# Keeping the activations token-major: weights as the moving operand, 512 columns wide, in a two-layer decoder trunk

## The chip, the cores and the metric

The kernel runs on one core of one Trainium2 chip. The metric is the device time of one execution in microseconds (us); lower is better. The kernel before was timed three times, and the profile shows one further execution.

## What is computed

The reference is a small decoder: 256 tokens of width 2048, two layers, everything in float32. Cut to what matters:

```python
for i in range(2):
    hn = rmsnorm(h, norm_mix[i])
    # layer 0: trailing means over tokens (windows 2, 4, 8, 16), then one 512x512 product per channel group
    # layer 1: differential attention, 8 heads: q, k, v from w_qkv, two softmaxes per head, rmsnorm, w_o
    h = h + (pool_mixer(hn, ...) if i == 0 else diff_attention(hn, ...))
    hn = rmsnorm(h, norm_ffn[i])
    h = h + (silu(hn @ w_gate[i]) * (hn @ w_up[i])) @ w_down[i]      # 2048 -> 5632 -> 2048
return rmsnorm(h, final_norm)
```

The weights are read once; the profile shows 350.96 MB read from HBM.

## The kernel before

**Precision.** A float32 product is carried by three passes in float32r. A weight tile w is split into `whi` (a cast, by ScalarE, L83) and `wlo` (w minus `whi`, by VectorE, L84); an activation x is split the same way into two halves [xh | xl] of one tile (`split`, L121 to L124). The passes are wh·xh, wl·xh and wh·xl.

**Layout.** The residual x is held feature-major: 16 tiles of 128 features by 256 tokens (`x_sb`). A product takes a 128x128 weight tile as TensorE's stationary operand and streams the activations through it. `product` (L89) makes one output tile of 128 features by 256 tokens in one PSUM bank: per weight tile a "big" matmul (L95) streams the 512 columns [xh | xl] through `whi` into both halves of the bank, and a "small" one (L98) streams the 256 columns xh through `wlo` onto the left half. I call the two a pair. The halves are added later, by a copy on ScalarE and an add on VectorE (`join`, L173).

Two products are token-major already: the group products of the pooling mixer and the v projection. `token_product` (L139) holds 128 tokens of xh or xl stationary and streams 512 weight columns: three matmuls (L147, L148, L149) of 512 columns for each 128 tokens and 128 rows of weights.

**Order of the work.** `Stream.unit` (L76) loads weights in chunks of 512 KB through SyncE's queue, four buffers deep, and splits each chunk once it is needed. The program is written stage by stage; a scheduler in the tile framework then fixes one static order for each engine, and the engines meet through semaphores. The stages are:

- the start (L182 to L268): x is loaded feature-major. Group 0 of the mixer's four channel groups is multiplied in plain float32 (L221), the others by `token_product`; `group_mean` (L243) scales by the norm, applies the trailing means with matmuls against a band matrix (L251 to L253) and adds to x;
- a feed-forward block, `ffn` (L270), run twice: 44 output tiles of gate and of up (16 pairs each, L278 and L285), joined, scaled by the norm's row `r`, silu, product, split into the 44 tiles `hT`; then 16 tiles of down (44 pairs each, L298), added to x;
- attention: q and k by `product` (32 tiles, L340), scores, softmax, transposed probabilities `aT` (L323); then for each of four 512-column parts of v a `token_product` (L399), and behind it for the two heads of that part the product of probabilities and v (L405 to L407), a norm per head (L411 to L415: two squares, `rsqrt`, two scalings `o_n`), four transposes by TensorE (L419), and the split into the operand `oT`; then w_o by `product` (L425);
- the final norm and the store (L433 to L440).

The norms need sums over features, which lie on partitions here: `norm_scale` (L152) gets them by matmuls with a tile of ones (L157) and spreads the result over partitions by four more (L164).

PSUM has eight banks of 128x512: five (`acc`) hold products, three (`aux`) everything else.

Of the kernel before, what the change touches and what calls it, by code (L numbers as in the profile page):

```python
# [9 lines left out]
F32 = mybir.dt.float32  # L10
# [6 lines left out]
P = 128  # L17
S = 256
D = 2048
NK = D // P  # L20
DFF = 5632
NF = DFF // P
# [3 lines left out]
CU = 8  # L26
WARM = 10
PLAIN = 1
WINDOWS = (2, 4, 8, 16)
HALO = 16  # L30
# [3 lines left out]


@with_exitstack
def trunk_kernel(ctx, tc, x_t, gains, subln, lam_in, band, dist,
                 pool_w, w_qk, w_v, w_o, w_gate, w_up, w_down, out):
# [12 lines left out]
    acc_ps = ctx.enter_context(tc.tile_pool(name="acc_ps", bufs=5, space=PSUM))  # L51
    aux_ps = ctx.enter_context(tc.tile_pool(name="aux_ps", bufs=3, space=PSUM))

# [9 lines left out]

    x_all = resid.tile([P, NK, S], F32, name="x_all")
    x_sb = [x_all[:, k, :] for k in range(NK)]
    xg = [resid.tile([P, 2, S], F32R, name=f"xg{k}") for k in range(NK)]

    def f32(ap):
        return ap.bitcast(F32)

# [1 line left out]
    class Stream:  # L72
        def __init__(self, w):
            self.w, self.next, self.have = w, 0, {}

        def unit(self, u):  # L76
            c = u // CU
            if c not in self.have:
                raw = wraw.tile([P, CU * P], F32, name="raw")
                nc.sync.dma_start(out=raw, in_=self.w[c])  # L80
                hi = whl.tile([P, CU * P], F32R, name="whi")
                lo = whl.tile([P, CU * P], F32R, name="wlo")
                nc.scalar.copy(hi, raw)  # L83
                nc.vector.tensor_tensor(lo, raw, f32(hi), ALU.subtract)  # L84
                self.have = {c: (hi, lo)}
            hi, lo = self.have[c]
            return hi, lo, (u % CU) * P

    def product(stream, u0, acts):  # L89
        """One output tile: units u0.. of the stream against acts; a bank [left | right]."""  # L90
        ps = acc_ps.tile([P, 2, S], F32, name="acc")
        n = len(acts)
        for k, a in enumerate(acts):
            hi, lo, at = stream.unit(u0 + k)
            big = lambda: nc.tensor.matmul(  # L95
                ps.rearrange("p a s -> p (a s)"), hi[:, at:at + P],
                a.rearrange("p a s -> p (a s)"), start=(k == 0), stop=(k == n - 1))
            small = lambda: nc.tensor.matmul(  # L98
                ps[:, 0, :], lo[:, at:at + P], a[:, 0, :], start=False, stop=False)
            if k < n - 1:  # L100
                big()
                small()
            else:
                small()
                big()
        return ps

    def rsqrt(ss, n, cols):
        """(ss / n + eps) ** -0.5 of [128, cols] sums, with one Newton step behind the
        square root's table."""  # L110
        v, s, t, r = (tmp.tile([P, 8], F32, name=f"rs_{x}") for x in "vstr")
        v, s, t, r = v[:, :cols], s[:, :cols], t[:, :cols], r[:, :cols]
        nc.vector.tensor_scalar(v, ss, 1.0 / n, EPS, ALU.mult, ALU.add)
        nc.scalar.activation(s, v, AF.Sqrt)
# [3 lines left out]
        nc.vector.scalar_tensor_tensor(r, t, 1.5, s, ALU.add, ALU.mult)  # L118
        return r

    def split(dst, src, gain):  # L121
        """dst = [hi | lo] of src * gain (gain by partition)."""
# [3 lines left out]
    def square_sum(k, ssq):  # L126
        if k == 0:
            nc.scalar.activation(ssq, x_sb[k], AF.Square)
        else:
            sq = tmp.tile([P, S], F32, name="sq")  # L130
            nc.scalar.activation(sq, x_sb[k], AF.Square)
            nc.vector.tensor_tensor(ssq, ssq, sq, ALU.add)

    def add_residual(k, ps):
        t = tmp.tile([P, S], F32, name="res_t")
        nc.vector.tensor_tensor(t, ps[:, 0, :], x_sb[k], ALU.add)
        nc.vector.tensor_tensor(x_sb[k], ps[:, 1, :], t, ALU.add)

    def token_product(stream, u0, acts):  # L139
        """[tokens, 512] in two banks: acts stationary against 512 columns of the stream."""  # L140
        ps = [acc_ps.tile([P, 512], F32, name="acc") for _ in range(2)]
        n = len(acts)
        for k, a in enumerate(acts):
            hi, lo, at = stream.unit(u0 + 4 * k)
            for t in range(2):
                xh, xl = a[:, 0, t * P:(t + 1) * P], a[:, 1, t * P:(t + 1) * P]
                nc.tensor.matmul(ps[t], xh, hi[:, at:at + 512], start=(k == 0), stop=False)  # L147
                nc.tensor.matmul(ps[t], xh, lo[:, at:at + 512], start=False, stop=False)  # L148
                nc.tensor.matmul(ps[t], xl, hi[:, at:at + 512], start=False, stop=(k == n - 1))  # L149
        return ps  # L150

    def norm_scale(ssq, rows=True):  # L152
        """Each token's rsqrt(mean square): by partition [128, 2], and [128, S] on every one."""
        ps = aux_ps.tile([P, 512], F32, name="aux")
        for t in range(2):
            for i, sq in enumerate(ssq):
                nc.tensor.matmul(ps[:, 2 * t:2 * t + 2], sq[:, t * P:(t + 1) * P], ones[:, 0:2],  # L157
                                 start=(i == 0), stop=(i == len(ssq) - 1))
        col = rsqrt(ps[:, 0:4:2], D, 2)
        if not rows:  # L160
            return col, None
        bc = aux_ps.tile([P, 512], F32, name="aux")
        for t in range(2):
            nc.tensor.matmul(bc[:, t * P:(t + 1) * P], col[:, t:t + 1].broadcast_to([P, P]), ident, start=True, stop=True)  # L164
        return col, bc

    def row_scale(ssq):
        col, bc = norm_scale(ssq)
        r = tmp.tile([P, S], F32, name="r_row")
        nc.scalar.copy(r, bc[:, :S])  # L170
        return col, r

    def join(ps, name):  # L173
        """left + right halves of a bank, in SBUF."""
        c = tmp.tile([P, S], F32, name=f"{name}_c", tag="join_c")
        nc.scalar.copy(c, ps[:, 1, :])  # L176
        s = tmp.tile([P, S], F32, name=f"{name}_s", tag="join_s", bufs=3)
        nc.vector.tensor_tensor(s, ps[:, 0, :], c, ALU.add)  # L178
        return s

# [1 line left out]
    with tc.tile_pool(name="start", bufs=1, reuse_waits="tile") as st:  # L182
        band_sb = st.tile([P, 4, P + HALO + P], F32, name="band_sb")
        pool_stream = Stream(pool_w)
# [4 lines left out]
        wp = aux_ps.tile([P, 512], F32, name="aux")  # L189
# [3 lines left out]
        def load_x(k0, k1):  # L193
            nc.sync.dma_start(out=x_all[:, k0:k1, :], in_=x_t[:, k0 * S:k1 * S].rearrange("p (k s) -> p k s", s=S))

        # the first groups' products in plain float32, which wait for no split
        zp = [None] * 4
        x0 = st.tile([P, 4 * PLAIN, S], F32, name="x0")
        w0 = []

        def load_w(c):
            raw = st.tile([P, CU * P], F32, name=f"w_plain{c}")
            nc.sync.dma_start(out=raw, in_=pool_w[c])
            w0.extend([raw[:, 0:512], raw[:, 512:]])

        load_x(0, 1)
        load_w(0)
        load_x(1, 4)
        load_w(1)
        for g in range(1, 4):  # L210
# [303 lines left out]
```

## Time and profile before

| what | value |
|---|---|
| time, median of 3 runs | 1941.9 us (1940.9 to 1942.17) |
| the profiled execution: first to last instruction (its span) | 1939.9 us |
| difference between that span and the median time | 2.0 us |
| TensorE (PE) busy | 1923.3 us, 99% of the span |
| VectorE (DVE) busy | 1187.4 us, 61% |
| ScalarE (ACT) busy | 938.8 us, 48% |
| DMA | 354.86 MB, mean 183 GB/s |

A matmul's row in the profile lasts from its start to a modelled end, and rows of successive matmuls overlap; how fast TensorE goes is read from start to start. PEld is the loading of stationary operands, which runs beside the matmuls. `PEclk` is the clock that TensorE was granted, 1.00 being full speed. The engine names with a q (SPq, DVEq, PEq) are the engines' instruction queues. The execution's own device time was not recorded apart from its span, so the work below adds the 2.0 us between that span and the median.

### The profile page before, as it was taken

How to read it: one execution, taken by the hardware profiler on the slowest of the kernel's cores; microseconds unless marked ns; L12 is line 12 of the kernel's file. 1: busy time of each engine (PE TensorE's matmuls, PEld its weight loads, DVE VectorE, ACT ScalarE, POOL GpSimd, SP SyncE). 2: the span in 40 equal slices, each digit the busy share in tenths (PEclk: the TensorE clock that was granted, in tenths of full speed). 3: DMA queues.
4: the chain of work that ended last, by engine and by line, in shares of the span. 5: the costliest groups of instructions: out<-in, count | busy, mean ns of one | idle time of the engine just before them, and what ended most of it. 6: DMA issues, size and time to landing. Idle time of an engine off the chain costs nothing.

```text
span 1939.9 us, 27612 instructions
## 1 busy us (share of the span) xinstructions
PE 1923.3 (99%) x10786; PEld 1664.6 (86%) x10786; DVE 1187.4 (61%) x1722; ACT 938.8 (48%) x1379; POOL 0.7 (0%) x6
## 2 busy tenths in 40 slices
PE   9999999999999999999999999999999999999997
PEld 7888888888888888888888888888888888888886
DVE  7766666666655555666655676666666666555554
ACT  7544444454444444544455545454544445444442
POOL 0000000000000000000000000000000000000000
PEclk9999999999999999999999999999999999999999
DMA  6666666656666665555555466665666665666663
GB/s 203 193 186 187 189 184 190 185 184 188 186 190 185 189 190 187 174 174 174 175 178 168 160 188 182 188 185 186 185 189 183 190 187 185 187 190 188 186 188 115
DMA packets 99330, 354.86 MB, mean 183 GB/s; under 512 B 11264, under 2 KB 13568, under 8 KB 99200
## 3 DMA queue, kind: packets, MB, share of 16 engines
q1 hardware_dynamic: 97984, 352.01, 59.4%
q8 instruction: 84, 1.38, 0.3%
q10 hardware_dynamic: 1216, 1.10, 0.2%
q14 instruction: 46, 0.38, 0.1%
HBM read 350.96 MB, written 2.10 MB: 182 GB/s over the span
## 4 chain that ended last, share of the span: by engine, by line
PE 98%; DVE 1%; ACT 0%; DMA 0%; issue 0%; SPq 0%; DVEq 0%
PE acc L95 60%; PE acc L98 30%; PE acc L148 2%; PE acc L149 2%; PE acc L147 2%; PE aux L376 1%; DMA x_all<-x_t 0%; PE aux L419 0%; PE aux L252 0%; DVE y_out L437 0%; PE aux L405 0%; PE aux L251 0%; DVE wlo L84 0%; PE aux L406 0%; PE aux L407 0%; ACT sq_in L227 0%
## 5 line engine op out<-in xcount | busy, mean ns | idle before, releaser
L95 PE MATMUL acc<-xg,whi 128*128 128x512 f32 x3328 | 1164.3, 399 | 0.0
L84 DVE TENSOR_TENSOR wlo<-raw,whi 128x1024 fp32r<-128x1024 f32 x662 | 810.1, 1224 | 475.0 <-ACT whi L83 459.4
L83 ACT CAST whi<-raw 128x1024 fp32r<-128x1024 f32 x662 | 694.7, 1050 | 506.6 <-PE acc L95 436.9
L98 PE MATMUL acc<-xg,wlo 128*128 128x256 f32 x3328 | 902.4, 281 | 0.0
L95 PEld LDWEIGHTS acc<-xg,whi 128*128 128x128 f32 x3328 | 612.6, 188 | 134.2
L98 PEld LDWEIGHTS acc<-xg,wlo 128*128 128x128 f32 x3328 | 628.3, 189 | 20.0
L95 PE MATMUL acc<-h,whi 128*128 128x512 f32 x1408 | 492.1, 394 | 0.0
L98 PE MATMUL acc<-h,wlo 128*128 128x256 f32 x1408 | 390.5, 281 | 0.0
L95 PEld LDWEIGHTS acc<-h,whi 128*128 128x128 f32 x1408 | 262.6, 188 | 59.6
L98 PEld LDWEIGHTS acc<-h,wlo 128*128 128x128 f32 x1408 | 264.0, 188 | 2.9
L176 ACT COPY g_c<-acc 128x256 f32<-128x256 f32 x88 | 32.7, 372 | 166.8 <-PE acc L95 166.8
L176 ACT COPY u_c<-acc 128x256 f32<-128x256 f32 x88 | 32.7, 372 | 166.4 <-PE acc L95 166.4
L178 DVE TENSOR_TENSOR u_s<-acc,u_c 128x256 f32<-128x256 f32 x88 | 37.3, 424 | 92.0 <-ACT u_c L176 92.0
L178 DVE TENSOR_TENSOR g_s<-acc,g_c 128x256 f32<-128x256 f32 x88 | 37.3, 424 | 90.0 <-ACT g_c L176 90.0
L95 PE MATMUL acc<-oT,whi 128*128 128x512 f32 x256 | 89.2, 396 | 0.0
L98 PE MATMUL acc<-oT,wlo 128*128 128x256 f32 x256 | 69.1, 282 | 0.0
L147 PE MATMUL acc<-whi,xg 128*128 128x512 f32 x152 | 60.5, 400 | 2.6 <-ACT whi L83 2.6
L148 PE MATMUL acc<-wlo,xg 128*128 128x512 f32 x152 | 61.7, 406 | 0.7 <-DVE wlo L84 0.7
L149 PE MATMUL acc<-whi,xg 128*128 128x512 f32 x152 | 61.0, 401 | 0.0
L95 PEld LDWEIGHTS acc<-oT,whi 128*128 128x128 f32 x256 | 47.1, 188 | 9.9
L290 ACT CAST h<-h 128x256 fp32r<-128x256 f32 x88 | 35.8, 407 | 39.6 <-DVE h L289 39.6
L98 PEld LDWEIGHTS acc<-oT,wlo 128*128 128x128 f32 x256 | 48.1, 188 | 1.5
(109 smaller groups left out, 751.6 us busy)
## 6 DMA issues: line engine op xcount, KB each, us to landing
raw<-w_gate SPq DMA_DIRECT2D x176, 512.0 KB, 4.1
raw<-w_up SPq DMA_DIRECT2D x176, 512.0 KB, 3.7
raw<-w_down SPq DMA_DIRECT2D x176, 512.0 KB, 4.3
raw<-w_qk SPq DMA_DIRECT2D x64, 512.0 KB, 3.6
raw<-w_v SPq DMA_DIRECT2D x32, 512.0 KB, 3.6
raw<-w_o SPq DMA_DIRECT2D x32, 512.0 KB, 4.3
raw<-pool_w SPq DMA_DIRECT2D x6, 512.0 KB, 7.0
x_all<-x_t SPq DMA_DIRECT2D x3, 512.0 KB, 7.5
```

The costliest lines, as they stand in the source:

```text
L83: nc.scalar.copy(hi, raw)
L84: nc.vector.tensor_tensor(lo, raw, f32(hi), ALU.subtract)
L95: big = lambda: nc.tensor.matmul(ps.rearrange("p a s -> p (a s)"), hi[:, at:at + P], a.rearrange("p a s -> p (a s)"), start=(k == 0), stop ...
L98: small = lambda: nc.tensor.matmul(ps[:, 0, :], lo[:, at:at + P], a[:, 0, :], start=False, stop=False)
L147: nc.tensor.matmul(ps[t], xh, hi[:, at:at + 512], start=(k == 0), stop=False)
L148: nc.tensor.matmul(ps[t], xh, lo[:, at:at + 512], start=False, stop=False)
L149: nc.tensor.matmul(ps[t], xl, hi[:, at:at + 512], start=False, stop=(k == n - 1))
L176: nc.scalar.copy(c, ps[:, 1, :])
L178: nc.vector.tensor_tensor(s, ps[:, 0, :], c, ALU.add)
L290: nc.scalar.copy(hT[j][:, 0, :], h)
L376: nc.tensor.matmul(sc[:, :nk], qk[:, c, qb * P:(qb + 1) * P], qk[:, 2 + c, :nk], start=True, stop=True)
```

## The change

The residual becomes token-major: `x_tok`, [128 tokens, 2 token blocks, 2048]. All products except q and k take the form that only v and the mixer had: activations stationary, 512 weight columns moving. Line numbers in this section are those of the changed kernel.

- **Products.** `group` computes 256 tokens by two blocks of 512 columns, in four banks at once: C11, C12 (first 128 tokens, left and right columns), C21, C22 (the other tokens). One step takes 256 rows of weights, one load of 1 MB in place of two of 512 KB, and 24 matmuls of 512 columns (L164). Three weight buffers in place of four, each twice as large; a split is one instruction of 128x2048 (L110, L111). A constant `SEVEN` for another variant is empty here, so its branches don't run.
- **Banks.** The four sums of `group` always lie in banks 6, 4, 5 and 7 (C11, C12, C21, C22); `aux` rotates over 5, 6 and 7, `acc` (q, k, mixer) over 0 to 4.
- **Feed-forward.** Gate and up stand side by side, 512 columns of each per group, 11 groups a layer. The result `h` has tokens on partitions, so it is turned back by eight transposes per group (L361) before it is split (L363, L364). The 11 groups are taken in three parts (4, 4, 3), each followed by its part of down (two groups), which is added to `x_tok`.
- **Norms.** A token's sum of squares is now along the free axis: ScalarE squares with an accumulated sum (`square_sum`); no matmuls with ones. The scale is applied per partition.
- **Operands.** Where a block needs x as stationary operand, `transposed` turns it by TensorE, 8 transposes for each 512 columns (L236), and splits.
- **Attention.** v comes in two groups of 1024 columns in place of four of 512, and behind each stand four heads in place of two.
- **Start and end.** x is loaded twice: feature-major for the mixer's products (2 MB) and token-major (2 MB); the pool scale (1 MB) and the final gain come broadcast over partitions. The mean over tokens is a matmul of 512 columns against the band matrix. The output is stored token-major.

The diff, cut to its core:

```diff
-    wraw = ctx.enter_context(tc.tile_pool(name="wraw", bufs=4))
-    whl = ctx.enter_context(tc.tile_pool(name="whl", bufs=4))
+    wraw = ctx.enter_context(tc.tile_pool(name="wraw", bufs=3))
+    whl = ctx.enter_context(tc.tile_pool(name="whl", bufs=3))
...
+    def load(src):
+        raw = wraw.tile([P, 4, 512], F32, name="raw")
+        nc.sync.dma_start(out=raw, in_=src)
+        return raw
+
+    def halves(raw, lo_block=0):
+        hi = whl.tile([P, 4, 512], F32R, name="whi")
+        lo = whl.tile([P, 4, 512], F32R, name="wlo")
+        nc.scalar.copy(hi[:, lo_block:], raw[:, lo_block:])
+        nc.vector.tensor_tensor(lo[:, lo_block:], raw[:, lo_block:], f32(hi[:, lo_block:]), ALU.subtract)
+        return hi, lo
...
+    def group(steps, seven_pool=None):
...
+                plan.append([(C11, [((0, 0), 0, B11), ((1, 0), 0, B21)]), (C12, [((0, 0), 0, B12), ((1, 0), 0, B22)]),
+                             (C21, [((0, 1), 0, B11), ((1, 1), 0, B21)]), (C22, [((0, 1), 0, B12), ((1, 1), 0, B22)])])
...
+                        ah, al = (a[:, k, i, t * P:(t + 1) * P] for i in range(2))
+                    for x, y in ((ah, hi), (ah, lo), (al, hi)):
+                        left[b] -= 1
+                        nc.tensor.matmul(ps[b], x, y[:, block], start=first, stop=(left[b] == 0))
...
+    def square_sum(ss, t, j):
+
+        sq = tmp.tile([P, 512], F32, name="sq", bufs=1)
+        nc.scalar.activation(sq, x_tok[:, t, j * 512:(j + 1) * 512], AF.Square, accum_out=ss[:, t, j:j + 1])
...
+    def transposed(xp, j, gain, seven=()):
+
+        for p in (2 * j, 2 * j + 1):
+            ps = aux((P, 2, 2, P))
...
+                    nc.tensor.transpose(ps[:, i, at], x_tok[:, t, cols], ident)
...
+                    split(xp[p][:, i], ps[:, i].rearrange("p t s -> p (t s)"), g[i])
...
+            for c, n in enumerate(CHUNKS):
...
+                for g in range(g0, g0 + n):
+                    ps = group([(xq[p], p in seven, w_gu[layer][g, p]) for p in range(NP)], hp)
+                    cs = combined(ps, hp)
+                    h = hp.tile([P, 2, 512], F32, name="h")
+                    for t in range(2):
+                        a = cs[t][0] if seven else hp.tile([P, 512], F32, name="silu", bufs=2)
+                        nc.scalar.activation(a, cs[t][0], AF.Silu, scale=r[:, t:t + 1])
+                        nc.vector.scalar_tensor_tensor(h[:, t], cs[t][1], r[:, t:t + 1], a, ALU.mult, ALU.mult)
+                    for i in range(2):
+                        ht = hp.tile([P, 2, 2, S], F32R, name=f"h{g - g0}_{i}")
+                        tp = aux((P, 2, S))
...
+                        nc.scalar.copy(ht[:, :, 0], tp)
+                        nc.vector.tensor_tensor(ht[:, :, 1], tp, f32(ht[:, :, 0]), ALU.subtract)
...
+                    ps = group([(hp_tiles[i], False, w_down[layer][o, 2 * g0 + i]) for i in range(2 * n)])
...
+                            nc.vector.tensor_tensor(x_tok[:, t, cols], cs[t][b], x_tok[:, t, cols], ALU.add)
...
-        for c in range(4):
-            cols = slice(c * 512, (c + 1) * 512)
-            vp = token_product(v_stream, c * NK * 4, xg)
...
-            for h in (2 * c, 2 * c + 1):
+        for g in range(2):
+            cs = combined(group([(xp[p], False, w_v[g, p]) for p in range(NP)]))
...
+            for h in range(4 * g, 4 * g + 4):
```

How the change moves TensorE's instructions is shown at two places. The first is the seam between one gate and up product and the next. In the kernel before, the next product (another `acc` bank) follows the last pair directly; this is the seam of two output tiles in the first feed-forward block, xg14 and xg15 being the last two feature tiles and xg0 the first.

```order
L95 MATMUL acc_1506<-xg14_102,whi_1531 128x512
L98 MATMUL acc_1506<-xg14_102,wlo_1532 128x256
L98 MATMUL acc_1506<-xg15_103,wlo_1532 128x256
L95 MATMUL acc_1506<-xg15_103,whi_1531 128x512
L95 MATMUL acc_1558<-xg0_88,whi_1561 128x512
L98 MATMUL acc_1558<-xg0_88,wlo_1562 128x256
```

In the changed kernel, TensorE at the first such seam of the first feed-forward block (b7_484 is C22 of the group that ends, h_701 its result, b4_737, b7_751, b5_744 and b6_730 are C12, C22, C21 and C11 of the next group; xp_93 and xp_94 are its first two steps):

```order
L164 MATMUL b7_484<-whi_673,xp_100 128x512
L361 MATMUL b5_709<-ident_77,h_701 128x128
L361 MATMUL b6_717<-ident_77,h_701 128x128
L164 MATMUL b4_737<-whi_726,xp_93 128x512
L164 MATMUL b4_737<-wlo_727,xp_93 128x512
L164 MATMUL b4_737<-whi_726,xp_93 128x512 x2
L361 MATMUL b5_709<-ident_77,h_701 128x128 x3
L361 MATMUL b6_717<-ident_77,h_701 128x128 x3
L164 MATMUL b4_737<-wlo_727,xp_93 128x512
...
L164 MATMUL b7_751<-whi_726,xp_93 128x512
...
L164 MATMUL b5_744<-whi_726,xp_93 128x512
```

Eight transposes now stand between the products, and the next group starts in the one bank (4) that they do not use; banks 5 and 6 follow once the transposed `h` has been read out of them.

The second place is behind a v product. Before, TensorE goes on with the next part of v (acc_9631, acc_9632) while a head is on its way through ScalarE and VectorE: the head's products with v (L405 to L407), twenty v matmuls, then the head's transposes (L419).

```order
L149 MATMUL acc_9420<-whi_9549,xg15_103 128x512
L147 MATMUL acc_9631<-whi_9635,xg0_88 128x512
L405 MATMUL aux_9567<-v_sb_7304,aT0_7686 128x256
L406 MATMUL aux_9567<-v_sb_7304,aT0_7686 128x256
L407 MATMUL aux_9567<-v_sb_7304,aT0_7686 128x256
L148 MATMUL acc_9631<-wlo_9636,xg0_88 128x512
...
L149 MATMUL acc_9631<-whi_9653,xg3_91 128x512
L419 MATMUL aux_9589<-ident_80,o_n_9586 128x128
L405 MATMUL aux_9599<-v_sb_7304,aT1_7946 128x256
```

In the changed kernel, TensorE behind the first v group (b7_6812 is its C22; b4_7174 is C12 of the second v group, the only bank of it that the heads leave free, taken three steps ahead):

```order
L164 MATMUL b7_6812<-whi_7001,xp_438 128x512
L517 MATMUL b5_7033<-v_sb_4861,aT0_5204 128x256
...
L517 MATMUL b7_7065<-v_sb_4861,aT1_5440 128x256
...
L164 MATMUL b4_7174<-whi_7227,xp_433 128x512
L531 MATMUL b6_7055<-ident_77,o_n_7052 128x128 x4
L531 MATMUL b5_7087<-ident_77,o_n_7084 128x128 x4
L517 MATMUL b6_7097<-v_sb_4861,aT2_5676 128x256
...
L517 MATMUL b5_7129<-v_sb_4861,aT3_5912 128x256
...
L531 MATMUL b7_7119<-ident_77,o_n_7116 128x128 x4
L531 MATMUL b6_7151<-ident_77,o_n_7148 128x128 x4
L164 MATMUL b5_7181<-whi_7163,xp_431 128x512
```

Eighteen matmuls of bank 4 stand between the first two heads' products and their transposes; between those and the transposes of heads 2 and 3 stand only the products of these heads, and none of the v product.

More of the change, by code (lines that the diff above doesn't have):

```diff
@@ L69, in f32 @@
         return ap.bitcast(F32)
[L72 to L87, printed above, removed]
@@ L139, in token_product @@
[L139 to L150, printed above, removed]
@@ L152, in norm_scale @@
[L152 to L165, printed above, removed]
@@ L188, in trunk_kernel @@
         nc.scalar.activation(warm[:, 0:1], ones[:, 0:1], AF.Sqrt)
[L189 removed]
+        wp = aux()
         for _ in range(WARM):
@@ new lines, in trunk_kernel @@
+        load_x(1, 4)
+        nc.sync.dma_start(out=w0[:, 2:4], in_=pool_w[0][:, 2:4])
+        load_x(4, 8)
+        x0 = st.tile([P, 4, S], F32, name="x0")
+        zp = [None] * 4
+        zp[0] = [acc() for _ in range(2)]
+        for k in range(4):
+            nc.vector.tensor_scalar(x0[:, k, :], xf[:, k], gain_sb[:, 0, k:k + 1], None, ALU.mult)
+            for t in range(2):
+                nc.tensor.matmul(zp[0][t], x0[:, k, t * P:(t + 1) * P], w0[:, k], start=(k == 0), stop=(k == 3))
@@ L333, in transpose_probs @@
             aT.append(a_t)
+        acts = [tile_of(xp, k) for k in range(NK)]
         probs = None
@@ L443, in _chunks @@
-def _chunks(w):
-    return w.reshape(P, -1, CU * P).transpose(1, 0, 2)
+                    split(oT[h][:, e], tp[:, e, :], gs[:, e:e + 1])
+        xq = operand(SEVEN)
+        for g in range(2):
+            cs = combined(group([(oT[p], False, w_o[g, p]) for p in range(NP)]))
+            for b in range(2):
+                j = 2 * g + b
+                cols = slice(j * 512, (j + 1) * 512)
+                for t in range(2):
+                    nc.vector.tensor_tensor(x_tok[:, t, cols], cs[t][b], x_tok[:, t, cols], ALU.add)
+                    square_sum(ss_next, t, j)
+                transposed(xq, j, 4, SEVEN)
```

476 lines of the change are left out of this document (279 added, 197 removed).

## The prediction

> **What bounds the kernel now.** I read the page first: engine shares and the chain that ended last.
>
> ```profile
> span 1939.9 us, 27612 instructions
> PE 1923.3 (99%) x10786; PEld 1664.6 (86%) x10786; DVE 1187.4 (61%) x1722; ACT 938.8 (48%) x1379; POOL 0.7 (0%) x6
> PE 98%; DVE 1%; ACT 0%; DMA 0%; issue 0%; SPq 0%; DVEq 0%
> ```
>
> TensorE is the chain for 98% of the span; nothing else is worth a stage's time. What counts is how fast its matmuls follow each other, and where it will have to wait. Pairs first, by the big matmul of each pair, in three clean stretches (gate and up, down, w_o; columns: stretch, length, busy and count of PE, of PEld, clock, DMA):
>
> ```profile
> 1192.00:1655.00 463.00, 456.62 (x1311) 240.54 (x1311) 1.00 0.62 186
> 1692.00:1915.00 223.00, 221.88 (x636) 118.36 (x636) 1.00 0.60 184
> 1100.00:1178.00 78.00, 76.91 (x223) 40.73 (x223) 1.00 0.62 189
> ```
>
> A pair takes 463/1311 = 0.3532 us in gate and up, 223/636 = 0.3506 in down, 78/223 = 0.3498 for w_o. The form that replaces them stands in the same trace: the v product, here the first and the last of 45 matmuls in a row without a gap in the timeline.
>
> ```profile
> 999.63 0.39 PE L148 MATMUL acc<-wlo,xg 128*128 128x512 f32 x1
> ...
> 1009.60 0.39 PE L147 MATMUL acc<-whi,xg 128*128 128x512 f32 x1
> ```
>
> 44 steps in 9.97 us: 0.2266 us for 512 columns. A pair is worth 1.5 of them, 0.340 us.
>
> **The change part by part.** *Products.* Gate and up are 2 x 88 x 16 = 2816 pairs, down 2 x 16 x 44 = 1408, w_o 256: 2816 x 0.3532 + 1408 x 0.3506 + 256 x 0.3498 = 1577.8 us. After: 280 steps of 24 matmuls, 6720 x 0.2266 = 1522.8. **-55 us.** This is the firm gain; q, k and v keep their matmuls. The Trainium skill, "TensorE: Matmul & The Clock Gate", section "Back-to-back issue gap", gives an isolated gap of N/2.4 + 2.5 ns, 216 ns at 512 columns, and less in a stream. By 216 ns the estimate of the gain would be 126 us instead of 55; the trace's 0.2266 us, with both operands in this kernel's own format, decides.
>
> *Splits and loads.* Twice the size, half as many.
>
> ```profile
> L84 DVE TENSOR_TENSOR wlo<-raw,whi 128x1024 fp32r<-128x1024 f32 x662 | 810.1, 1224 | 475.0 <-ACT whi L83 459.4
> L83 ACT CAST whi<-raw 128x1024 fp32r<-128x1024 f32 x662 | 694.7, 1050 | 506.6 <-PE acc L95 436.9
> L401 ACT ACTIVATE v_sb<-acc,r_col 128x512 f32<-128x512 f32 x8 | 5.5, 687 | 3.9 <-PE acc L149 3.9
> L230 DVE TENSOR_TENSOR ssq_in<-ssq_in 128x512 f32<-128x512 f32 x1 | 0.7, 681 | 0.0
> L124 DVE SCALAR_TENSOR_TENSOR xg<-x_all,gain_sb,xg 128x256 fp32r<-128x256 f32 x60 | 28.3, 477 | 0.1
> ```
>
> From 681 ns for 512 and 1224 for 1024 I extend to 2.3 us for a VectorE split of 2048, and likewise (687, 1050) to 1.9 on ScalarE. A step needs 4.2 of the 5.44 us (24 x 0.2266) that TensorE takes, on two engines, and three buffers let a split run two steps ahead. The load is 1 MB per 5.44 us, 193 GB/s, where 186 flow now. Zero.
>
> *22 gate and up seams.* Each adds eight transposes. Single and double ones stand among the v matmuls now:
>
> ```profile
> 991.74 0.40 PE L148 MATMUL acc<-wlo,xg 128*128 128x512 f32 x1
> 991.98 0.27 PE L330 MATMUL aux<-ident,a_sb 128*128 128x128 f32 x1
> ...
> 992.32 0.40 PE L147 MATMUL acc<-whi,xg 128*128 128x512 f32 x1
> ...
> 994.14 0.40 PE L149 MATMUL acc<-whi,xg 128*128 128x512 f32 x1
> 994.38 0.38 PE L330 MATMUL aux<-ident,a_sb 128*128 128x128 f32 x2
> ...
> 994.83 0.39 PE L148 MATMUL acc<-wlo,xg 128*128 128x512 f32 x1
> ```
>
> Two matmuls and one transpose take 0.58 us instead of 0.453, with two 0.69: 0.12 us a transpose, 0.95 for eight. Do they wait? Let T be the end of C22. VectorE finishes `h` of the first tokens before T and of the second at T + 0.9 (one 512-column operation after C22); TensorE reaches the transposes that need it at T + 1.1, after two transposes and four matmuls of bank 4. The read-out of the transposed `h` is queued behind the split of step three ahead on both engines (1.9, then 2.3 from T + 0.2), so bank 5 is free at T + 5.2; by the order shown, TensorE has matmuls of banks 4 and 7 until T + 5.0. I put 0.2 us of wait (0 to 0.8). Queued behind it is all of the next group. 22 x 1.15 = **+25 us** (21 to 38). Down's seams add no transposes, and their four adds (0.7 each) are done bank by bank before TensorE asks: zero.
>
> The Trainium skill, same page, "Part 4: PE-mode transpose", speaks against the change: about 275 ns for a transpose in a kernel. The trace's row lasts 0.27 too, but its place in the stream costs 0.12.
>
> *Operand transposes.* 64 outside the start x 0.12 = **+7 us**, and at the four half seams where x must be added, turned and split with only bank 4 or one q product to run meanwhile, I count a wait of about 1.3 us each (splits of 0.48 us, four in a row, against 18 matmuls): **+5** (2 to 8). The norms' matmuls leave:
>
> ```profile
> L157 PE MATMUL aux<-ones,ssq 128*128 128x2 f32 x16 | 2.3, 230 | 0.0
> ```
>
> With the wait on them I take **-2**; their work goes to ScalarE's squares, which have room.
>
> *Heads behind v.* One head's way today:
>
> ```profile
> 1092.91 0.59 PE L407 MATMUL aux<-v_sb,aT 128*128 128x256 f32 x2
> 1093.60 0.38 ACT L411 ACTIVATE o_sq<-aux 128x256 f32<-128x256 f32 x1 [0.43 <-PE aux L407]
> 1094.24 0.20 ACT L411 ACTIVATION_READ_ACCUMULATOR o_sq<-aux 128x1 f32 x1
> 1094.47 0.17 DVE L113 TENSOR_SCALAR rs_v<-o_ss 128x2 f32<-128x2 f32 x1
> 1094.85 0.19 ACT L114 ACTIVATE rs_s<-rs_v 128x2 f32<-128x2 f32 x1
> 1095.97 0.16 DVE L118 SCALAR_TENSOR_TENSOR rs_r<-rs_t,rs_s 128x2 f32<-128x2 f32 x1
> 1096.17 0.84 ACT L415 ACTIVATE o_n<-aux,rs_r 128x256 f32<-128x256 f32 x2 [1.12 <-DVE rs_r L118]
> ```
>
> From the last product (1093.5) to both o_n (1097.0) 3.5 us, all covered by v or w_o matmuls today. After the change `aux` and the group share banks 5 to 7, so only 18 matmuls of bank 4 (4.1 us) cover anything. A head's products cost 1.22 us:
>
> ```profile
> 1009.86 0.70 PE L405 MATMUL aux<-v_sb,aT 128*128 128x256 f32 x2
> ...
> 1011.08 0.58 PE L148 MATMUL acc<-wlo,xg 128*128 128x512 f32 x1
> ```
>
> From T: products of two heads to 2.4, cover to 6.6. ScalarE reads v (0.7) and splits 2048 (1.9) first, to T + 2.9; four squares and the norm put the first transposes at 8.2: 1.6 idle, 0.4 more for the second head. Heads 2 and 3 need those banks, free after four splits each way: 1.5 idle. Then products, and the chain again with only the other head's 1.2 us beside it: 2.0, and 1.4 for the last head. About 7 us, in two places: **+13.5** (5 to 19).
>
> *Start.* Down begins here, and DMA and clock look so:
>
> ```profile
> 545.57 0.39 PE L95 MATMUL acc<-h,whi 128*128 128x512 f32 x1
> 10.00:15.00 5.00, 2.62 (x7) 0.84 (x5) 4.59 (x7) 5.00 (x9) 0.00 (x0) 1.00 1.02 407
> 15.20:22.00 6.80, 6.06 (x17) 4.66 (x18) 4.29 (x8) 3.76 (x8) 0.00 (x0) 0.55 0.89 306
> 15.25 0.74 PE L147 MATMUL acc<-whi,xg 128*128 128x512 f32 x2 [2.63 <-ACT whi L83]
> ```
>
> Less 1408 x 0.3532 for gate and up, the start costs 545.6 - 497.3 = 48.3 us today. After: SyncE's queue carries 5.8 MB up to the end of token-major x, which at 407 GB/s lands at 18; eight squares (0.69) and the norm (1.7, from rs_v to o_n above) give r at about 25.5. From there VectorE has in its queue: 8 scalings and 8 adds of 512 (0.7), five splits (2.3), 20 half splits (0.48), the norm (1): 33 us, to 58.5, and 0 to 5 of waiting; 18 matmuls (4.1 us) of the first group have run by then. 57 against 48.3: **+9** (5 to 14).
>
> *End.*
>
> ```profile
> 1926.03 0.40 PE L95 MATMUL acc<-h,whi 128*128 128x512 f32 x1
> 1930.70 4.74 DVE L437 TENSOR_TENSOR y_out<-x_all,aux 128x256 f32<-128x256 f32 x6 [0.80 <-PE aux L164]
> ```
>
> 13.9 us from the last matmul. After: add, square, norm 3.7, eight scalings 5.7, the same store: zero (-1 to +1).
>
> *Clock.* In the start, TensorE idles 2.63 us and then runs at 0.55 for 6.8 us. In each head place, the last 4.35 us before v or w_o go on hold 0.9 us of transposes and no matmul. I take a half-clock stretch behind each, worth 2.5 us of its possible 3.4: **+5** (0 to 12). By the Trainium skill, same page, Part 1, it takes an idle window of about 3.4 us, free-running; one idle gap here is shorter, so by that rule alone the clock could stay: the second rival.
>
> **Sum.** -55 + 25 + 7 + 5 - 2 + 13.5 + 9 + 0 + 5 = +7.5. On the span 1947.4; with the 2.0 us between it and the median, **1949 us**.
>
> **The rivals.**
>
> - *The head places are free* (0.22). If ScalarE and VectorE run two heads side by side so that bank 4 covers the first pair and the second pair's chains hide in each other, 18.5 us go (13.5 and the clock's 5): **1931**, faster. It turns to faster once these places cost under 7 us in all. For it: 1.12 and 0.43 us of ScalarE's chain above are waits. Against: the banks.
> - *Full clock throughout* (0.26). No 5: **1944**, no change. For: transposes in between. Against: the row at 15.20.
> - *The read-outs of h come later* (0.12). If the split queued ahead of them starts 0.6 us later than I count, TensorE waits at each of 22 seams: +13, **1962**. It decides from the 0.2 us that I found as slack there.
> - *Transposes cost their full row* (0.03): 240 x (0.27 - 0.12) = +36, **1985**. Against: the rows above.
>
> The forecast has 0.37.
>
> **How the numbers follow.** About 0.2%, 3.9 us, is what a measurement of this kernel can tell from no change: 1938.0 to 1945.8. Full clock lies inside with 0.20 of its 0.26, 0.03 on either side. Faster 0.22 + 0.03 = 0.25; same 0.20; slower 0.37 + 0.12 + 0.03 + 0.03 = 0.55. The range takes in the free head places below (1930) and the late read-outs with some of the start's bound above (1966); the rest is left out.
>
> **What would show it.** L164 matmuls 0.2266 us apart in feed-forward, 5.44 us a step; transposes 0.12. Idle at each L361 seam about 0.2 us; about 7 us behind each v group, ended by L527 and L226; the first group in full swing at about 57 + 4 us; `PEclk` 0.5 behind a v group or not. Wrong if the L164 spacing differs by 2 ns (13 us), or if idle stands at every step, which would mean splits or loads bind.

## The result, and the profile after

The changed kernel takes 1955.5 us (median of four runs, 1954.2 to 1955.68) against 1941.45 of the kernel before beside it (1940.9 to 1942.17): 14.1 us more, a ratio of 1.0072 with a 95% interval of 1.0058 to 1.0086. The forecast was slower by 7.5 with 1949 us; the profiled span grew by 13.9, from 1939.9 to 1953.8. The sign and most of the mechanisms held, and one term of the sum failed by 18 us. First the head of the page after: the span, TensorE's busy time and the chain.

```profile
span 1953.8 us, 20579 instructions
PE 1920.1 (98%) x8706; PEld 1565.5 (80%) x8706; DVE 965.0 (49%) x859; ACT 799.2 (41%) x770; POOL 0.7 (0%) x6
PE 95%; DVE 2%; ACT 1%; DMA 1%; issue 0%; SPq 0%; DVEq 0%; ACTq 0%
```

Instructions fell by a quarter, VectorE went from 61% to 49%, and TensorE is still the chain: it has 2080 matmuls fewer and is about as long at work. So splits and loads bind nowhere behind the start, as forecast: the loads of L164's stationary operands waited for a `wlo` for 1.3 us in all, and for a `whi` not at all. The question is again how fast the matmuls follow each other. Three stretches that hold nothing but L164, first gate and up (stationary `xp`), then down (`h`), then w_o (`oT`); columns: stretch, length, busy and count of PE, clock, DMA.

```profile
110.00:145.00 35.00, 35.00 (x156) 1.00 0.53 185
245.00:320.00 75.00, 75.00 (x323) 1.00 0.53 182
1120.00:1152.00 32.00, 32.00 (x139) 1.00 0.58 197
```

A row lasts 0.39 us, so the count holds those that began up to 0.39 before the stretch. 35.39/156 is 0.2269 us, 75.40/323 is 0.2334, 32.40/139 is 0.2331. From the starts of all L164 matmuls in the trace (gaps over 0.26 us left out) the means are 0.2270 for `xp`, 0.2333 for `h` and 0.2333 for `oT`. Gate and up go as forecast. Down and w_o, 2112 + 384 matmuls, are 6.7 ns slower each: 16.7 us. It is the same line, the same form and the same full clock.

A seam of gate and up, TensorE's timeline:

```profile
101.58 0.39 PE L164 MATMUL b<-whi,xp 128*128 128x512 f32 x1
101.81 0.38 PE L361 MATMUL b<-ident,h 128*128 128x128 f32 x2
101.94 0.47 PE L164 MATMUL b<-whi,xp 128*128 128x512 f32 x1
102.26 0.39 PE L164 MATMUL b<-wlo,xp 128*128 128x512 f32 x1
102.49 0.63 PE L164 MATMUL b<-whi,xp 128*128 128x512 f32 x2
102.96 0.81 PE L361 MATMUL b<-ident,h 128*128 128x128 f32 x6
103.53 0.47 PE L164 MATMUL b<-wlo,xp 128*128 128x512 f32 x1
103.84 0.62 PE L164 MATMUL b<-whi,xp 128*128 128x512 f32 x2
```

From 101.58 to 103.84 stand six L164 matmuls, 1.36 us, and eight transposes: 0.90 for those. With what the next groups of rows lose, the 22 seams cost 1.07 on average by the starts in the trace (1.15 forecast). The first group ends at 101.81; less 192 x 0.2267 the start costs 58.3 us against 48.3, +10 (9 forecast).

The place behind the first v group, TensorE's timeline from the first head products on:

```profile
1037.22 0.59 PE L517 MATMUL b<-v_sb,aT 128*128 128x256 f32 x2
...
1039.62 0.58 PE L164 MATMUL b<-whi,xp 128*128 128x512 f32 x1
...
1043.71 0.39 PE L164 MATMUL b<-whi,xp 128*128 128x512 f32 x1
1044.24 1.64 PE L531 MATMUL b<-ident,o_n 128*128 128x128 f32 x8
1047.45 0.67 PE L517 MATMUL b<-v_sb,aT 128*128 128x256 f32 x2 [1.57 <-DVE oT L226]
...
1049.68 0.59 PE L519 MATMUL b<-v_sb,aT 128*128 128x256 f32 x2
1051.71 0.91 PE L531 MATMUL b<-ident,o_n 128*128 128x128 f32 x4 [1.43 <-ACT o_n L527]
1053.55 1.27 PE L531 MATMUL b<-ident,o_n 128*128 128x128 f32 x4 [0.93 <-ACT o_n L527]
1054.47 0.78 PE L164 MATMUL b<-whi,xp 128*128 128x512 f32 x1
```

This is the forecast's picture: products of two heads, the 18 matmuls of bank 4 as cover, then TensorE waits for `oT` (whose read-out frees the banks) and twice for `o_n`. Of the 17.25 us from 1037.22 to 1054.47, cover is 4.1, products 4.9, transposes 16 x 0.12 = 1.9; 6.3 are idle (about 7 forecast). The second place, behind the second v group, lasts 16.9 us from 1094.99 to 1111.90; less 18 x 0.2333 = 4.2 of cover and the same 4.9 and 1.9, 5.9 are idle. The clock behind the first place, once that stretch is over, and behind the second (columns as above):

```profile
1053.00:1056.00 3.00, 2.45 (x8) 0.52 0.00 0
1057.00:1060.00 3.00, 3.00 (x15) 1.00 0.00 0
1111.50:1114.50 3.00, 3.00 (x9) 0.50 0.00 0
```

Half clock came behind each place, as forecast; the records show 3.4 us of it each time. It held five matmuls behind the first place and six behind the second at about 0.43 instead of 0.23, which cost 1.1 and 1.3 us, where 2.5 were forecast for each.

### The profile page after: what moved, and what is told of

The parts are those of the page before. It is cut to its first block, busy times and chain, and to the rows that moved or that the text cites. A ratio compares the mean times of both kernels' runs of the same rounds, so it can differ in the third digit from the quotient of the medians.

```text
span 1953.8 us, 20579 instructions
## 1 busy us (share of the span) xinstructions
PE 1920.1 (98%) x8706; PEld 1565.5 (80%) x8706; DVE 965.0 (49%) x859; ACT 799.2 (41%) x770; POOL 0.7 (0%) x6
## 4 chain that ended last, share of the span: by engine, by line
PE 95%; DVE 2%; ACT 1%; DMA 1%; issue 0%; SPq 0%; DVEq 0%; ACTq 0%
PE b L164 82%; PE b L418 6%; PE b L420 3%; PE b L361 1%; DMA x_tok<-x_n 1%; DVE wlo L111 1%; PE b L299 1%; PE b L485 1%; ACT sq L214 0%; PE b L309 0%; ACT whi L110 0%; PE b L531 0%; PE b L236 0%; DVE xp L226 0%; ACT o_sq L523 0%
## 5 line engine op out<-in xcount | busy, mean ns | idle before, releaser
L111 DVE TENSOR_TENSOR wlo<-raw,whi 128x2048 fp32r<-128x2048 f32 x331 | 758.4, 2292 | 837.4 <-ACT whi L110 837.4
L110 ACT CAST whi<-raw 128x2048 fp32r<-128x2048 f32 x331 | 633.6, 1915 | 940.5 <-PE b L164 933.2
L164 PE MATMUL b<-whi,xp 128*128 128x512 f32 x3072 | 955.7, 391 | 0.0
L164 PEld LDWEIGHTS b<-whi,xp 128*128 128x128 f32 x3072 | 577.1, 188 | 125.7 <-DVE h L364 4.5
L164 PE MATMUL b<-wlo,xp 128*128 128x512 f32 x1536 | 600.4, 391 | 0.0
L164 PE MATMUL b<-whi,h 128*128 128x512 f32 x1408 | 445.2, 396 | 0.0
L164 PEld LDWEIGHTS b<-wlo,xp 128*128 128x128 f32 x1536 | 288.8, 188 | 58.6 <-DVE wlo L111 0.5
L164 PEld LDWEIGHTS b<-whi,h 128*128 128x128 f32 x1408 | 264.5, 188 | 65.2 <-DVE h L364 1.4
L164 PE MATMUL b<-wlo,h 128*128 128x512 f32 x704 | 279.0, 396 | 0.0
L418 PE MATMUL b<-xp,whi 128*128 128x512 f32 x512 | 182.8, 401 | 0.0
L164 PEld LDWEIGHTS b<-wlo,h 128*128 128x128 f32 x704 | 132.3, 188 | 31.1 <-DVE wlo L111 0.4
L164 PE MATMUL b<-whi,oT 128*128 128x512 f32 x256 | 82.7, 401 | 0.0
L164 PEld LDWEIGHTS b<-whi,oT 128*128 128x128 f32 x256 | 48.7, 190 | 11.9 <-issue 0.3
L164 PE MATMUL b<-wlo,oT 128*128 128x512 f32 x128 | 51.1, 399 | 0.0
```

Of the source, the lines that this page charges most:

```text
L110: nc.scalar.copy(hi[:, lo_block:], raw[:, lo_block:])
L111: nc.vector.tensor_tensor(lo[:, lo_block:], raw[:, lo_block:], f32(hi[:, lo_block:]), ALU.subtract)
L164: nc.tensor.matmul(ps[b], x, y[:, block], start=first, stop=(left[b] == 0))
L418: big = lambda: nc.tensor.matmul(ps.rearrange("p a s -> p (a s)"), hi[:, k], a.rearrange("p a s -> p (a s)"), start=(k == 0), stop=(k == N ...
```

## The experiments

Line numbers move by one to three where an edit adds lines: L165, L166 and L167 below are the L164 of the changed kernel. Spacings are means from the starts in the trace, gaps over 0.26 us left out. Byte addresses are those of the built program, within a partition of SBUF, the memory of all tiles but the accumulators. e5, e6, e7 and e9 to e12 were executed once each; the four executions of the changed kernel lie within 1.5 us. `...` marks lines left out of a diff, and comments behind `#` are added here.

**First question: why are `h` and `oT` slower?** Nothing in the instruction differs, so the first suspects were addresses. The split weights begin at byte 64 within 128, and so does `xp`; `h` at 96, `oT` at 0.

*e1, `h` and `oT` moved to 64 within 128 by padding:*

```diff
+            pad = hp.tile([P, 24], F32, name="pad")        # ahead of the feed-forward tiles
+            nc.gpsimd.memset(pad, 0.0)
...
+        pad = ap_.tile([P, 16], F32, name="pad")           # ahead of q, k and oT
+        nc.gpsimd.memset(pad, 0.0)
```

> The changed kernel, with 96 bytes of padding ahead of the feed-forward tiles and 64 ahead of the attention's oT tiles, so that every operand that L164 holds stationary begins at the same place within 128 bytes as the weights (64), as xp already does; h began at 96, oT at 0. Theory 1 (that place sets the spacing): the 2112 + 384 matmuls with h and oT go from 0.2333 to 0.2267 us apart, 16.5 us less, span about 1937, time about 1939. Theory 2 (the spacing comes from where in SBUF the tiles lie, far above the weights, or from the order of the products): still 0.2333, time 1955 to 1956.

Measured: 1955.0 us, span 1953.3, ratio to before 1.0071 (1.0054 to 1.0088). `h` 0.2327, `oT` 0.2323. In this form the theory fell: the spacing moved by 0.6 and 1 ns, not by 6.7. That it moved at all showed that addresses have a say.

*e6, `h` and `oT` laid out low, behind `xp`; e7, `xp` laid out high, behind the weights:*

```diff
 e6
+    acts_low = ctx.enter_context(tc.tile_pool(name="acts_low", bufs=1))    # ahead of wraw and whl
-                        ht = hp.tile([P, 2, 2, S], F32R, name=f"h{g - g0}_{i}")
+                        ht = acts_low.tile([P, 2, 2, S], F32R, name=f"hT{g - g0}_{i}", tag=f"a{2 * (g - g0) + i}")
...
-                oT[h] = ap_.tile([P, 2, 2, S], F32R, name=f"oT{h}", tag="qk", bufs=8)
+                oT[h] = acts_low.tile([P, 2, 2, S], F32R, name=f"oT{h}", tag=f"a{h}")
...
 e7
+    opnd = ctx.enter_context(tc.tile_pool(name="opnd", bufs=1))            # behind wraw, whl and tmp
+    pad = opnd.tile([P, 24], F32, name="pad")
-        return [resid.tile(...
+        return [opnd.tile(...
```

> The changed kernel with the tiles of the turned h and of oT (and q, k, which share them) laid out right behind xp, from byte 52,800 of each partition to 85,568, below the weights, which move up to 85,568 to 159,296; before they lay at 137,312 to 178,304, above the weights. Theory 1 (L164's spacing comes from where in SBUF the stationary operand lies): h and oT go from 0.2333 to 0.2267 us, about 16 us less, span about 1937. Theory 2 (it comes from the products themselves: their order, their number of steps, what else runs): still 0.2333, span 1953 to 1955.

> The changed kernel with xp moved up behind the weights, to bytes 96,448 to 129,216, and the weights down to 20,032 to 93,760; h stays where it was, within 96 bytes. Theory 1a (an operand above the weights is loaded more slowly): the 4608 matmuls with xp go from 0.2270 to 0.2333 us, 29 us more, span about 1983. Theory 1b (it is the upper part of SBUF, beyond 131,072, that is slow): xp stays at 0.2267, span 1953 to 1955. Theory 2 (the products themselves): no change either; the run with h and oT laid low tells it from 1b.

Measured: e6 span 1938.2 (15.6 less), `h` 0.2269, `oT` 0.2272. e7 span 1978.7 (24.9 more), `xp` 0.2327. The same products changed their pace both ways with their place alone, so theory 2 fell. The groups show it in the mean row as well; first `xp` and `h` of the changed kernel, then `hT` (the turned h) of e6, then `xp` of e7.

```profile
L164 PE MATMUL b<-whi,xp 128*128 128x512 f32 x3072 | 955.7, 391 | 0.0
L164 PE MATMUL b<-whi,h 128*128 128x512 f32 x1408 | 445.2, 396 | 0.0
```

```profile
L165 PE MATMUL b<-whi,hT 128*128 128x512 f32 x1408 | 436.6, 390 | 0.0
```

```profile
L167 PE MATMUL b<-whi,xp 128*128 128x512 f32 x3072 | 970.8, 396 | 0.0
```

390 or 391 ns is the fast pace and 396 the slow one. I read this as "above the weights is slow" (1a), and the next two runs put that to the test.

*e9, the split weights below `xp`, which stands where e6's `h` stood; e10, `xp` still higher, across the place where a bound would have to lie:*

```diff
 e9
+    whl = ctx.enter_context(tc.tile_pool(name="whl", bufs=3))
+    opnd = ctx.enter_context(tc.tile_pool(name="opnd", bufs=1))            # xp
     resid = ctx.enter_context(tc.tile_pool(name="resid", bufs=1))
     wraw = ctx.enter_context(tc.tile_pool(name="wraw", bufs=3))
-    whl = ctx.enter_context(tc.tile_pool(name="whl", bufs=3))
...
 e10
+    whl = ctx.enter_context(tc.tile_pool(name="whl", bufs=3))
+    wraw = ctx.enter_context(tc.tile_pool(name="wraw", bufs=3))
+    opnd = ctx.enter_context(tc.tile_pool(name="opnd", bufs=1))            # xp
     resid = ctx.enter_context(tc.tile_pool(name="resid", bufs=1))
-    wraw = ctx.enter_context(tc.tile_pool(name="wraw", bufs=3))
-    whl = ctx.enter_context(tc.tile_pool(name="whl", bufs=3))
...
```

> The changed kernel with the split weights moved down to bytes 3,648 to 52,800 of each partition and xp behind them, at 52,800 to 85,568: the very place where h and oT were fast while the weights lay above them. h and oT stay at 137,312 and up. Theory 1a (what counts is whether the stationary operand lies below or above the streamed one): xp goes to about 0.2328 to 0.2333, span 1978 to 1984. Theory 1c (what counts is the stationary operand's own place, with a bound between 85,568 and 96,448): xp stays at 0.2267 to 0.2270, span 1953 to 1955. In both h and oT stay at 0.2333.

> The changed kernel with xp laid across the region in which a bound must lie by the runs so far: xp's eight tiles from byte 77,376 to 110,144, the split weights at 3,648 to 52,800, the loaded ones between. Theory 1c (a bound of the stationary operand's own place): within one and the same group the tiles below the bound run at 0.2267 and those above at about 0.2327, with one step somewhere between 85,568 and 96,448; with the bound in the middle some 60% of 4608 matmuls are slow, 17 us more, span 1968 to 1974 (1961 to 1979 for the ends). Theory 1d (each group runs at one rate, set by something else in the layout): all tiles alike, span 1953 to 1955 or 1978 to 1981.

Measured: e9 span 1953.3, `xp` 0.2270, which ended 1a. e10 span 1953.5, `xp` 0.2270 in all eight tiles, up to byte 110,144, which ended 1c too: the stretch from 96,448 to 110,144 was slow in e7 and is fast here. `h` and `oT`, left in place, stayed at 0.2333 to 0.2335 in both.

```profile
L165 PE MATMUL b<-whi,xp 128*128 128x512 f32 x3072 | 956.9, 392 | 0.0
```

Laid side by side, the operands of all these runs sort themselves by one number, the distance of the stationary operand's start from the weights' start within 512 bytes: 0 in every fast one, 32, 64, 128 or 160 in every slow one. e7's tiles had been 128 off. So the first theory came back in a wider form.

*e11, that distance made 0 with `h` and `oT` left high above the weights; e12, everything shifted by 64, and `h` put at a distance of 256:*

```diff
 e11
+            pad = hp.tile([P, 120], F32, name="pad")       # h up by 480 bytes
...
+        pad = ap_.tile([P, 112], F32, name="pad")      # oT up by 448
...
 e12
+    pad = resid.tile([P, 16], F32, name="pad")             # ahead of x_tok: all up by 64
...
+            pad = hp.tile([P, 56], F32, name="pad")        # h up by a further 224
...
```

> The changed kernel with h and oT above the weights where they were, moved up by 480 and 448 bytes, so that they begin at the same place within 512 bytes as the weights (64); before, h began at 96 and oT at 128. In every run so far, xp, h or oT is fast where it begins at the weights' place within 512, and slow at 32, 64, 128 or 160 bytes from it; where it lay in SBUF otherwise (the run with xp from 77,376 to 110,144 was fast throughout) made no difference. Theory 3 (the place within 512 bytes, relative to the streamed operand): h and oT at 0.2267, 15 to 17 us less, span 1937 to 1939. Theory 1 (where in SBUF, high or above the weights): still 0.2333, span 1953 to 1955.

> The changed kernel with everything behind the constants shifted by 64 bytes, so that xp and the weights both begin at 128 within 512, oT at 64 from them as before, and h by a further 224 at 256 from them. Theory 3a (the place relative to the weights counts, within 512): xp stays at 0.2267 to 0.2270, h and oT at 0.2320 to 0.2333, span 1953 to 1955. Theory 3b (the place itself counts, 64 within 512): xp goes to 0.2327 or more, span 1978 to 1982. Theory 3c (relative, but within 256 bytes): h goes to 0.2267, span 1939 to 1941.

Measured: e11 span 1941.4, `h` and `oT` 0.2270. e12 span 1939.7, `xp` 0.2270, `h` 0.2270, `oT` 0.2334. The same groups, of e11 and then of e12:

```profile
L164 PE MATMUL b<-whi,h 128*128 128x512 f32 x1408 | 437.0, 390 | 0.0
```

```profile
L166 PE MATMUL b<-whi,xp 128*128 128x512 f32 x3072 | 955.0, 391 | 0.0
L166 PE MATMUL b<-whi,h 128*128 128x512 f32 x1408 | 436.6, 390 | 0.0
L166 PE MATMUL b<-whi,oT 128*128 128x512 f32 x256 | 82.6, 401 | 0.0
```

(The 401 of `oT` is the slow pace with the matmuls at half clock behind the second head place averaged in; in the changed kernel its mean row is 401 too.) Theory 3c holds: the distance counts relative to the streamed operand (3b fell, since `xp` stayed fast at its new place), and within 256 bytes (`h` is fast at 256). e11 gained 12.4 where 16 were due; by the starts in its trace 1.7 of the rest were lost in the first head place, where the clock was halved twice (as in e5 below, whose first place costs as much), and about 1 in q and k, whose tiles its padding moved too. All runs together:

| operand and run | starts at byte | from the weights, within 256 | spacing, us |
|---|---|---|---|
| `xp`, changed kernel | 20,032 | 0 | 0.2270 |
| `h`, `oT`, e6 | 52,800 | 0 | 0.2269, 0.2272 |
| `xp`, e9 (weights below it) | 52,800 | 0 | 0.2270 |
| `xp`, e10 | 77,376 | 0 | 0.2270 |
| `h`, `oT`, e11 | 137,792 and 145,984 | 0 | 0.2270, 0.2270 |
| `h`, e12 | 137,600 | 0 (256) | 0.2270 |
| `h`, changed kernel | 137,312 | 32 | 0.2333 |
| `oT`, changed kernel and e12 | 145,536 and 145,600 | 64 | 0.2333, 0.2334 |
| `h`, `oT`, e1 | 137,408 and 145,600 | 128 | 0.2327, 0.2323 |
| `xp`, `h`, e7 | 96,448 and 137,408 | 128 | 0.2327, 0.2327 |
| `oT`, e7 | 145,632 | 160 | 0.2334 |

The layouts alone leave one rival. The loaded weights (`raw`), which the DMA writes and which ScalarE and VectorE read, begin in every run at the same place within 256 bytes as the split ones, so the distance could count relative to what these do beside TensorE. The trace of the changed kernel settles it: in the stretches between two starts in which neither engine has a row and no DMA packet is in flight, the mean spacing is 233.3 ns for `h` (225 of them) and 226.8 for `xp` (336).

**Second question: do the head places wait for banks?** *e3, a group's four accumulators in banks 0 to 3:*

```diff
-    M1, M6, M7, P5, P3, P4, M2, X = range(8)
+    P3, P4, M2, X, M1, M6, M7, P5 = range(8)
```

> The changed kernel with the four accumulators of a group in banks 0 to 3 instead of 4 to 7, so that they share none with transposes and head products (5 to 7). Theory 1 (the head places wait because all but one bank of the next group is held by the heads): TensorE runs the next group through the heads' chains, the two places lose nearly all of the about 6.5 us idle and the 1.5 us of half clock each; 14 to 17 us less, time 1939 to 1942. Theory 2 (ScalarE's and VectorE's queues set it: the splits are late behind the heads' work whatever the banks): under 4 us less, 1952 to 1956.

Measured: 1932.4 us, ratio to before 0.9954 (0.9939 to 0.9969); span 1930.8, 23.0 less than the changed kernel. First the two head places of the changed kernel as windows (here with all engines: PE, PEld, DVE, ACT, POOL, then clock, DMA), then those of e3.

```profile
1034.00:1060.00 26.00, 21.82 (x93) 16.93 (x93) 10.93 (x30) 16.15 (x43) 0.00 (x0) 0.93 0.27 95
1095.00:1120.00 25.00, 20.97 (x89) 16.05 (x88) 9.17 (x30) 14.75 (x39) 0.00 (x0) 0.93 0.23 84
```

```profile
1028.00:1054.00 26.00, 25.88 (x123) 21.32 (x122) 13.31 (x30) 18.70 (x43) 0.00 (x0) 1.00 0.48 171
1079.00:1104.00 25.00, 25.00 (x117) 19.87 (x116) 13.38 (x32) 17.92 (x43) 0.00 (x0) 1.00 0.38 136
```

With banks of their own the heads leave TensorE without a row for 0.12 us instead of 8.2 (rows overlap, so this is less than the idle time by the starts), the clock stays at 1.00, and the loads flow on. By the starts in the two traces the places lose 6.8 and 6.4 us less, 13.2 together, which is what bank sharing and half clock cost there. Nine of the other ten lay where I had not looked for them: the start 3.0, the 22 seams 0.18 each (4.0), three half seams 0.7 each (2.2). The transposes of `h` and of x stand in banks 5 to 7 as well. The rest is the first L164 matmul, which comes 0.65 us earlier in this trace; in e8, with the same banks, it does not.

**Third question: what does a seam cost?** *e5, no transposes of `h`:*

```diff
-                        tp = aux((P, 2, S))
...
-                                nc.tensor.transpose(tp[:, k, t * P:(t + 1) * P],
+                        tp = h[:, :, 2 * i * P:(2 * i + 2) * P].rearrange("p t (k s) -> p k t s", s=P)
...
```

> The changed kernel without the 176 transposes of h: the read-outs copy h's blocks unturned, so the feed-forward gives other numbers; the work of ScalarE and VectorE stays. Theory 1 (a seam costs eight transposes at 0.12 us and waits of 0.2 to 0.5): 22 seams save 1.1 to 1.4 us each, 24 to 31 us less, span 1923 to 1930. Theory 2 (the seam's cost is the wait for h and comes back at the next matmul): under 10 us less.

Measured: span 1930.6, 23.2 less, 1.05 us a seam. That is just under the 24 of theory 1's lower end and far from theory 2: all of the seam's cost is the transposes and what waits on them, and none comes back. The 23.2 is a net: in this trace the first L164 matmul comes 0.6 us earlier, and the first head place costs 1.6 more, with its clock halved twice there. Without these the seams are worth about 24.

**A version that beats both.** *e8, e6 and e3 together:*

> The changed kernel with both repairs: accumulators of a group in banks 0 to 3, and h and oT laid out below the weights. Theory 1 (the two losses are separate): 1955.5 less 23.1 and 15.6 as each gave alone, 1916 to 1918, 1.2% below the kernel before. Theory 2 (with faster products VectorE's or ScalarE's splits or the loads bind somewhere): part of the 15.6 comes back as waits, 1920 to 1928.

Measured: 1917.05 us (1916.72 to 1917.45) against 1941.07 before, ratio 0.9874 (0.9857 to 0.989). The two losses are separate: 1955.5 - 23.1 - 15.6 = 1916.8. The page of e8:

```profile
span 1915.7 us, 20553 instructions
PE 1893.0 (99%) x8706; PEld 1565.5 (82%) x8706; DVE 963.3 (50%) x859; ACT 796.8 (42%) x770; POOL 0.7 (0%) x6
```

Against the kernel before, the change with both repairs is 24.0 us faster; where tiles lay and which banks were shared had cost it 38.5.

## Why the prediction was right, and where it was not

| term | forecast, us | measured, us | from |
|---|---|---|---|
| gate and up | -37.4 | -35.8 | 4224 x 0.2270 against 994.6 |
| down and w_o | -17.6 | -0.9 | 2496 x 0.2333 against 583.2 |
| 22 seams | +25 | +23.5 | 1.07 each; e5 gives 23.2 |
| four half seams | +12 | about +10 | 2.5 each in three of them |
| head places, idle | +13.5 | +12.2 | 6.3 and 5.9 |
| head places, clock | +5 | +2.4 | 1.1 and 1.3 |
| start | +9 | +10 | 58.3 against 48.3 |
| end | 0 | -0.9 | 13.0 against 13.9 |
| norms | -2 | -6.6 | what is left of +13.9 |

- **The step that failed** is "6720 x 0.2266". The rate was taken from the v product of the kernel before, "with both operands in this kernel's own format", and given to all products. It holds for 4224 of the 6720; the other 2496 hold an operand stationary that starts 32 or 64 bytes off the weights, which in v it does not. So -55 became -36.7. e11 and e12 show the cause, and that it is the address and not the products. The prediction had named the sign itself: it is wrong if the spacing differs by 2 ns, 13 us in all. For down and w_o it differs by 6.7 ns, so this term, which it called the firm gain, was wrong there.
- **Splits and loads at zero**: right, no idle at every step; a split takes 2.29 us on VectorE and 1.92 on ScalarE, where 2.3 and 1.9 were estimated.
- **Seams**: right in kind and size; of the 1.07 us, the 0.18 that e3 takes away are the wait for banks, put at 0.2. The rival in which the read-outs of `h` come later (1962) fell, since 1.07 is below the 1.15 counted; that transposes cost their full row (1985) fell too, by the seam's rows and by e5.
- **Heads**: right, and for the reason given; e3 takes the banks away and the idle goes. The rival of free head places (1931) is what e3 made of the kernel, not what the change was. That e3 comes out at 1932 is luck: it lacks 18 us of the gain on products that the rival counts, and gains ten elsewhere.
- **Clock**: the half clock came, so the rival of full clock (1944) fell, but it cost half of what I put. I had taken the stretch of the start, 6.8 us at half clock, of which 3.4 could be lost; here it is 3.4 us long, so 1.7 could be lost, and 1.3 and 0.75 us of it were over before the 512-column matmuls went on. Nor does it come every time: the same two places in e6, e9, e10 and e12 show half clock at one only. What decides that was not tried. By the Trainium skill, "TensorE: Matmul & The Clock Gate", Part 1, the clock falls after an idle window of about 3.4 us. The trace disagrees with that if idle means no work at all: the longest single wait there was 1.57 us, and transposes stood between.
- **Start and end**: the start to within about a microsecond; 3.0 us of it are the wait for banks that e3 takes away, which the text had as 0 to 5 of waiting.
- **Norms**: the -2 was a guess from small rows, and the -6.6 is only what is left. Part of it is not the norms: from the first v matmul to the end of w_o (986.2 to 1180.8) the kernel before takes 194.6 us, about 3 more than its v and w_o matmuls, head products and transposes come to at the prediction's own prices. In its trace the first v matmul behind a head's products takes 0.42 us to the next start instead of 0.23, and the first behind its transposes 0.31. The sum put this price at nothing. The other 3 to 4 us are not told apart.

So the total is 6.4 us from the forecast because two errors met: 18.3 us that I had counted as gain on the products did not come, and the other terms together were put 11.9 too high. That the total came so near is luck.

## What to carry to other kernels

In this form of matmul, a spacing read from one product held for another only where its operands lay alike: before a rate is carried over, compare the addresses of both operands, and where two streams of TensorE run at slightly different pace in the same form, shift one tile so that their distance is a multiple of 256 bytes and look again. Before a stage is moved next to another, count who holds which PSUM bank, since four free banks were worth 23 us here. Work that a change puts in the way should be priced as rows in the stream, as the seams were, not by the length of a row.

## What was not expected of the hardware

For back-to-back matmuls of 128x128 by 512 in float32r, the spacing is about 227 ns (means of 226.9 to 227.2) where the stationary operand's start differs from the streamed one's by a multiple of 256 bytes, about 233.3 at a difference of 32, 64 or 160, and 232.3 to 232.7 at 128; other distances were not tried. The Trainium skill, "TensorE: Matmul & The Clock Gate", section "Back-to-back issue gap", says that in a stream the weight load and the matmul together set the spacing; that agrees in so far as the pace here depends on the places of both operands. The runs show only the rule and not what lies behind it. It is no rule for every form: in the kernel before, whose matmuls alternate between 512 and 256 columns, the pairs that stream `xg`, at a distance of 0 from their stationary weights, take 0.3524 us on average by the starts in the trace, and those that stream `h`, at 192, take 0.3510. Right behind a seam, many of `xp`'s matmuls take 229 to 236 ns for a few microseconds before they fall into 226 or 227; why was not tried either.
